# Sums of squares of an attention head: squares as stationary operand of two columns, or as moving operand of a constant

## The chip, the core and the metric

The kernel runs on one core of a Trainium2 chip. The metric is the device time of one execution in microseconds. The engines of the core are TensorE (matmul; PE and, for its weight loads, PEld in the profile), VectorE (DVE), ScalarE (ACT), GpSimd (POOL) and SyncE (SP), whose queue issues all DMAs here. Each engine works through its own instructions in the order in which the program gives them, and semaphores hold an instruction until its operands are there.

## The reference

The program is one layer of a mixer with two branches over 1152 tokens (1024 latent ones and 128 of context, nine tiles of 128). This case is about the end of the attention branch. For each of eight heads, with `va` of 128 columns a head:

```python
w = softmax(q1 @ k1.T) - lam * softmax(q2 @ k2.T)
oa = w @ v
oa = oa * lax.rsqrt(jnp.mean(jnp.square(oa), axis=-1, keepdims=True) + LN_EPS)
oa = oa * subln_g * (1.0 - lam_init)
oa = (oa * silu(za)) @ w_pa
```

The mean of squares is over the 128 columns of one head, so there is one factor per head and token.

## The kernel before

All matmul operands are float32. Most matmuls run in a faster float32 form (`F32R`), with each operand split into a rounded part (`hi_of`, a copy on ScalarE) and a remainder (`lo_of`, a subtraction on VectorE or GpSimd), and three products hi*hi, hi*lo, lo*hi. A matmul of plain float32 operands takes no split; the trace shows it as two weight loads and two matmuls.

The kernel writes its order out by hand. `Sched` (lines 38 to 136) is a planner at build time: it keeps an estimated TensorE time `sch.t` and estimated times at which ScalarE, VectorE and GpSimd come free, and runs generator streams. A stream yields the time (or a condition) at which it wants to go on; the first ready stream in the list emits its next instructions. Waits such as `yield sch.t + 4.0` only place instructions in the order; on the chip only semaphores count.

In the attention stage (`phase_b`) three streams run, in this priority: `softmax_stream`, `pv_stream`, and the dense stream. Streams that are added with `sch.spawn` go ahead of all.

- `softmax_stream` goes over the heads, in five chunks of queries each (four of 256, one of 128), in tiles of 128 queries. For both halves of the difference it writes scores into the one buffer of PSUM tag `S`, takes the maximum (line 1067, tile `nm`), then the exponential (tile `E`). `fin` combines the two halves; `eps` holds the term of each query that stands for `LN_EPS`.
- `pv_stream` (line 1106) transposes the weights of a chunk, splits them (`wTh`, `wTl`) and multiplies by V into PSUM `o`, with the head's 128 columns on partitions and queries along the free dimension. At the end of a chunk (from line 1171) it takes `Square` of `o` into `sq`, scales `o` into `o_sb`, and spawns `post`: for each 128 queries a matmul with `sq` as the stationary operand and `ones` (two columns of 1/128) as the moving one. Its result has queries on partitions, so that a copy puts it into a column of `ms`.
- `rms` (line 1080), one per head, waits for the fifth chunk, adds `eps`, takes the power -0.5 on GpSimd, transposes the nine columns to rows, stores them (`RSd`), loads them back over all partitions (`rb`, tag `rec`, two buffers, three loads of 384 queries) and scales `o_sb` with them on GpSimd. Then `done["attn", h]` is set.
- The dense stream (`dense`, line 322) takes jobs from `nxt` (line 1342): V of late heads, `z` (the gate `za` of an attention head, 12 us of matmul), `zr`, and 16 gate jobs. It loads and splits two jobs ahead. A `z` job is not placed before `done["attn", h]`; its result goes through `gate_out` (line 941): a tanh on ScalarE, a product, then on GpSimd the product with `o_sb`, then on ScalarE the split for the store. `gate_out` has two buffers `tz`, and dense jobs have two PSUM buffers `dn`. `spare` (line 1339) is the number of gate jobs that `nxt` holds back for after the last `z` job.

When the last head is scaled, `done["B"]` ends the stage. The dense stream goes on with what is left (`z` of head 7, the spare gates, then eight `pr` and eight `pa` jobs), while `x_loads` brings the `X` tiles, into the memory that the attention stage left, for the `pr` jobs.

Of the kernel before, what the change touches and what calls it, by code (L numbers as in the profile page):

```python
# [11 lines left out]
F32 = mybir.dt.float32  # L12
# [6 lines left out]
P = 128  # L19
# [3 lines left out]
NT = NL + P  # L23
# [116 lines left out]
def hybrid_step(ctx: ExitStack, tc: tile.TileContext, I: dict, O: dict):  # L140
# [5 lines left out]
    def mm(out, lhsT, rhs, start, stop):  # L146
        n = rhs.free_size()
        sch.t += max(n / 2400 + 0.013, 0.11) if lhsT.dtype == F32R else max(n / 600 + 0.01, 0.22)
        nc.tensor.matmul(out, lhsT=lhsT, rhs=rhs, start=start, stop=stop)  # L149
# [5 lines left out]
    def act(out, in_, func=AF.Copy, after=None, **kw):  # L155
        nc.scalar.activation(out, in_, func, **kw)  # L156
        extra = sum(not isinstance(v, (int, float)) for v in kw.values())
        return sch.op("act", 0.06 + out.free_size() / 1200 + 0.09 * extra, after)
# [4 lines left out]
    def v_tt(out, a, b, op, after=None):  # L163
        nc.vector.tensor_tensor(out, a, b, op=op)  # L164
        return sch.op("dve", 0.07 + out.free_size() / 960, after, in_sbuf(a, b))
# [18 lines left out]
    def p_tt(out, a, b, op, after=None):  # L184
        nc.gpsimd.tensor_tensor(out, a, b, op=op)  # L185
        return sch.op("pool", 0.2 + out.free_size() * (0.17 if op == ALU.pow else 0.00205), after, True)
# [15 lines left out]
    def dma(out, in_):  # L202
        nc.sync.dma_start(out=out, in_=in_)  # L203
# [8 lines left out]
    ONd = tc.dram_tile((NH, P, NT), F32, name="ONd")  # L212
    Gd = tc.dram_tile((16, P, NT), F32, name="Gd")
    Td = tc.dram_tile((8, P, NT), F32, name="Td")
    RSd = tc.dram_tile((NH, NTILE, P), F32, name="RSd")
    gated = tc.dram_tile((16, P), F32, name="gated")

# [12 lines left out]
    def room(tag):  # L230
        return sch.room(tag, PS[tag][1])

    def psum(tag, shape=(P, 512)):
        return PS[tag][0].tile(list(shape), F32, tag=tag, name=tag), sch.bank(tag)
# [8 lines left out]
    Y = big.tile([P, 2, KT, NT], F32R, name="Y")  # L243

    ident = const.tile([P, P], F32, name="ident")
    ones = const.tile([P, 2], F32, name="ones")
    mhalf = const.tile([P, 16], F32, name="mhalf")
    bg = const.tile([P, 16], F32, name="bg")
    bm = const.tile([P, 24], F32, name="bm")
# [109 lines left out]
    def phase_h(first, load_decays):  # L359
# [3 lines left out]
        with es:  # L363
# [42 lines left out]
            for i in range(1, NTILE):  # L406
                load_x(i)
            junk = p0.tile([P, D], mybir.dt.bfloat16, name="junk")
            nc.gpsimd.memset(ones, 1.0 / P)
            nc.gpsimd.memset(mhalf, -0.5)  # L410
            act(sc, cond, AF.Tanh, scale=0.5)
            v_stt(sc, sc, 1.0, cond, ALU.add, ALU.mult)
# [560 lines left out]
    def phase_b():  # L973
# [105 lines left out]

        def rms(h, o_sb, ms):  # L1080

            yield lambda: ms[1] if len(ms) == 2 else None
            rs = pb.tile([P, NTILE], F32, tag="rs", name="rs", bufs=2)
            f = v_tt(rs, ms[0], eps[h], ALU.add)
            yield p_tt(rs, rs, mhalf[:, :NTILE], ALU.pow, f)
            yield room("tp")
            tp, tok = psum("tp")
            tpose(tp[0:NTILE, :P], rs)
            rt = pb.tile([NTILE, P], F32, tag="rst", name="rst")
            tok[0] = act(rt, tp[0:NTILE, :P])  # L1090
            dma(RSd[h], rt)
            rb = []
            for c in range(NC):
                rb.append(pb.tile([P, CW], F32, tag="rec", name="rb", bufs=2))
                dma(rb[c], RSd[h, 3 * c:3 * c + 3].rearrange("t q -> (t q)").partition_broadcast(P))
                if c:
                    yield sch.t + (4.0 if c == 1 else 0.5)
                    for d in (c - 1, c) if c == 2 else (c - 1,):
                        if d == 2:
                            yield sch.t + 3.5  # L1100
                        cs = slice(d * CW, (d + 1) * CW)
                        f = p_tt(o_sb[:, cs], o_sb[:, cs], rb[d], ALU.mult)
            OS[h] = o_sb
            done["attn", h] = f

        def pv_stream():
# [4 lines left out]
            for h in range(NH):  # L1111
                yield lambda: 0.0 if h < 2 or ("gate_out", h - 2, True) in done else None
                o_sb = pz.tile([P, NT], F32, tag="o_sb", name="o_sb", bufs=2)
                ms = [pb.tile([P, NTILE], F32, tag="ms", name="ms", bufs=2)]
                sch.spawn(rms(h, o_sb, ms))
                for c in range(5):
                    if c == 1:
# [53 lines left out]
                    cs = slice(c * 256, c * 256 + n)  # L1171
                    yield lambda: 0.0 if state["sq"] == 0 else None
                    state["sq"] = 1
                    sq = pb.tile([P, 256], F32, tag="sq", name="sq", bufs=1)
                    act(sq[:, :n], o[:, :n], AF.Square)
                    otok[0] = act(o_sb[:, cs], o[:, :n], scale=subg)

                    def post(sq=sq, c=c, nq=nq, ms=ms, f=otok[0]):
                        yield f
                        yield room("tp")  # L1180
                        sp, tok = psum("tp")
                        for q in range(nq):
                            mm(sp[:, 2 * q:2 * q + 2], sq[:, q * P:(q + 1) * P], ones, True, True)
                        state["sq"] = 0
                        tok[0] = v_ts(ms[0][:, 2 * c:2 * c + nq], sp[:, 0:2 * nq:2], 1.0, None, ALU.mult)
                        if c == 4:
                            ms.append(tok[0])

                    sch.spawn(post())
            yield lambda: done.get(("attn", NH - 1))  # L1190
# [145 lines left out]
        zrs = list(range(NH))  # L1336
        prs = list(range(8))
        pas = list(range(8))
        spare = 2
        late_v = [4, 5, 6, 7]  # L1340

        def nxt():
# [28 lines left out]
        psum_pool(es, "tp", 2)  # L1371
        psum_pool(es, "S", 1)
        psum_pool(es, "o", 1)
        load_k(0)
        load_q(0, 0)
        sch.run([softmax_stream(), pv_stream(), stream], lambda: "B" in done)
# [251 lines left out]
```

## Time and profile before

| what | value |
|---|---|
| runs | 1703.99, 1703.97, 1699.94 us; median 1703.97 |
| profiled execution | 1701.82 us, span 1700.0 us |
| busy TensorE matmul / weight load | 97% / 95% of the span |
| busy VectorE, ScalarE, GpSimd | 50%, 36%, 48% |
| preparation and first products, 0 to 80 us | matmul busy 60.0 us |
| projections and retention, 80 to 600 us | 515.0 of 520 |
| attention with dense jobs, 600 to 1330 us | 720.7 of 730 |
| rest of dense jobs, 1389 to 1594 us | 201.7 of 205 |
| output projection, 1594 to 1700 us | 98.1 of 106 |

Views used below. The windows view has one row per stretch: its limits, its length, then busy time with number of instructions for PE, PEld, DVE, ACT and POOL, the granted TensorE clock, the busy share of the DMA engines and GB/s. The timeline has start, duration, engine, line, operation, what it writes and reads with shapes, and the number of merged instructions; in brackets stands how long the engine was idle before and who released it. Starts matter more than durations on TensorE, since matmuls overlap. The view of one tile lists the instructions that touch it, with shortest, median and longest duration in ns and the first and last start. A row of DMA issues has what it writes and reads, the number, KB each and the median time to landing.

### The profile page before, as it was taken

Reading aid. Unit: us, or ns where it says so; the run is one execution under the profiler, and the core shown is the slowest. Engines: PE = TensorE matmul, PEld = TensorE weight load, DVE = VectorE, ACT = ScalarE, POOL = GpSimd, SP = SyncE. Lnnn points to the kernel's source line nnn. Section 1 sums busy time; section 2 is a strip of 40 time slices with the busy share of each in tenths; the row PEclk is TensorE's granted clock in tenths of the full one; section 3 lists DMA queues with packets and bytes.
Section 4 is the critical chain, followed back from the end, with each engine's and each line's share of the span. In section 5 each row is a group of like instructions: output and inputs, shape, how many; then the busy total and the mean of one; then the engine's idle time right before and its main releaser. Section 6 shows DMA issues by size and latency. Waiting matters only on the chain.

```text
span 1700.0 us, 27027 instructions
## 1 busy us (share of the span) xinstructions
PE 1654.5 (97%) x10495; PEld 1609.5 (95%) x10495; DVE 856.3 (50%) x1681; ACT 609.6 (36%) x1138; POOL 813.1 (48%) x555
## 2 busy tenths in 40 slices
PE   6899999999999999999999999999999999999998
PEld 5699999999999999999999999999999999999886
DVE  8545506413714626665555665666565124134676
ACT  5632222121221235555555555555545220012200
POOL 4547417444634637664847475656656322112200
PEclk8999999999999999999999999999999999999999
DMA  7435412430341365443535353525242578854432
GB/s 274 149 100 147 131 46 86 132 116 23 100 127 44 112 204 161 152 144 113 169 97 172 92 167 93 170 95 165 75 158 73 202 273 282 260 174 137 160 125 87
DMA packets 135185, 237.36 MB, mean 140 GB/s; under 512 B 15801, under 2 KB 103313, under 8 KB 134033
## 3 DMA queue, kind: packets, MB, share of 16 engines
q1 hardware_dynamic: 135056, 235.63, 43.4%
q8 instruction: 83, 1.36, 0.3%
q14 instruction: 46, 0.37, 0.1%
HBM read 161.08 MB, written 74.49 MB: 139 GB/s over the span
## 4 chain that ended last, share of the span: by engine, by line
PE 80%; DVE 6%; DMA 5%; issue 3%; POOL 3%; ACT 2%; SPq 1%; DVEq 0%; POOLq 0%; ACTq 0%
PE dn L149 53%; PE S L149 8%; PE o L149 6%; PE e L149 6%; PE tp L153 4%; PE a L149 4%; DMA gt<-Gd 2%; DVE junk L173 1%; SPq L203 1%; DMA wm<-in_w_shift 1%; ACT E L156 1%; PE tp L149 1%; DVE st L181 1%; DVE eps L173 1%; POOL wlo L185 1%
## 5 line engine op out<-in xcount | busy, mean ns | idle before, releaser
L149 PE MATMUL dn<-Y,whi 128*128 128x384 f32 x3200 | 834.3, 341 | 8.7 <-ACT Y L156 2.8
L149 PEld LDWEIGHTS dn<-Y,whi 128*128 128x128 f32 x3200 | 568.1, 189 | 14.7 <-ACT Y L156 4.0
L149 PE MATMUL dn<-Y,wlo 128*128 128x384 f32 x1600 | 537.5, 336 | 0.7 <-DVE wlo L164 0.7
L185 POOL TENSOR_TENSOR wlo<-raw,whi 128x1024 fp32r<-128x1024 f32 x87 | 210.9, 2428 | 444.8 <-ACT whi L156 444.5
L149 PEld LDWEIGHTS dn<-Y,wlo 128*128 128x128 f32 x1600 | 301.5, 188 | 1.0 <-DVE wlo L164 1.0
L1067 DVE TENSOR_REDUCE nm<-S 128x1 f32<-128x1152 f32 x144 | 178.1, 1237 | 180.4 <-PE S L149 180.0
L189 POOL TENSOR_SCALAR E<-E,r 128x640 f32<-128x640 f32 x64 | 142.8, 2231 | 126.8 <-DVE r L173 86.2
L156 ACT ACTIVATE E<-S,nm 128x1152 f32<-128x1152 f32 x144 | 162.4, 1128 | 79.4 <-DVE nm L1067 73.5
L149 PE MATMUL dn<-whi,Y 128*128 128x256 f32 x864 | 157.4, 283 | 2.4 <-ACT rt L156 1.0
L149 PEld LDWEIGHTS dn<-whi,Y 128*128 128x128 f32 x864 | 134.1, 189 | 3.3 <-ACT rt L156 1.4
L149 PE MATMUL o<-wTh,V 128*128 128x256 f32 x576 | 133.6, 290 | 0.1
L156 ACT ACTIVATE wTh<-tp 128x512 fp32r<-128x512 f32 (+1 forms) x168 | 88.7, 544 | 111.4 <-PE tp L153 107.7
L156 ACT ACTIVATE whi<-raw 128x1024 fp32r<-128x1024 f32 x88 | 92.1, 1055 | 85.0 <-PE dn L149 84.8
L149 PE MATMUL dn<-wlo,Y 128*128 128x256 f32 x432 | 121.3, 281 | 0.0
L164 DVE TENSOR_TENSOR wTl<-tp,wTh 128x512 fp32r<-128x512 f32 (+1 forms) x168 | 99.7, 613 | 24.9 <-ACT wTh L156 24.9
L185 POOL TENSOR_TENSOR E<-E 128x640 f32<-128x640 f32 x64 | 100.9, 1576 | 5.3
L149 PE MATMUL S<-K,QH 128*128 128x384 f32 (+1 forms) x400 | 94.6, 340 | 5.8 <-ACT E L156 5.8
L149 PEld LDWEIGHTS o<-wTh,V 128*128 128x128 f32 x576 | 99.3, 188 | 0.5 <-ACT wTh L156 0.4
L149 PE MATMUL S<-K,QL 128*128 128x384 f32 (+1 forms) x400 | 92.5, 334 | 0.0
L153 PE MATMUL tp<-ident,E 128*128 128x128 f32 x584 | 86.8, 272 | 0.0
L173 DVE SCALAR_TENSOR_TENSOR gt<-gt,dn 128x384 f32<-128x384 f32 x48 | 26.6, 554 | 117.9 <-DMA gt<-Gd 64.7
L169 DVE TENSOR_SCALAR KD<-tp,kdec 128x256 f32<-128x256 f32 (+1 forms) x48 | 16.0, 408 | 138.5 <-PE tp L153 138.5
(197 smaller groups left out, 2504.4 us busy)
## 6 DMA issues: line engine op xcount, KB each, us to landing
K<-Kd SPq DMA_DIRECT2D x8, 1280.0 KB, 7.9
Gd<-gt SPq DMA_DIRECT2D x48, 192.0 KB, 2.3
V<-Vd SPq DMA_DIRECT2D x24, 384.0 KB, 3.6
gt<-Gd SPq DMA_DIRECT2D x48, 192.0 KB, 2.5
Y<-OAd SPq DMA_DIRECT2D x16, 576.0 KB, 4.2
raw<-in_w_gate SPq DMA_DIRECT2D x16, 512.0 KB, 4.0
QH<-Qh SPq DMA_DIRECT2D x64, 128.0 KB, 3.1
QL<-Ql SPq DMA_DIRECT2D x64, 128.0 KB, 2.9
```

Source lines behind the costliest of these rows:

```text
L149: nc.tensor.matmul(out, lhsT=lhsT, rhs=rhs, start=start, stop=stop)
L153: nc.tensor.transpose(out, in_, ident)
L156: nc.scalar.activation(out, in_, func, **kw)
L164: nc.vector.tensor_tensor(out, a, b, op=op)
L169: nc.vector.tensor_scalar(out, a, s1, s2, op0=op0, **kw)
L173: nc.vector.scalar_tensor_tensor(out, a, s, b, op0=op0, op1=op1, **kw)
L181: nc.vector.bn_stats(out, a)
L185: nc.gpsimd.tensor_tensor(out, a, b, op=op)
L189: nc.gpsimd.tensor_scalar(out, a, s1, None, op0=op0)
L203: nc.sync.dma_start(out=out, in_=in_)
L1067: nc.vector.tensor_reduce(nm[:, m:m + 1], ps[:, :nb, :kw], axis=AX.XY, op=ALU.max, negate=True)
```

## The change

The squares are no longer the stationary operand. `Square` goes to a float32 tile `s2`; `hi_of` and `lo_of` split it into the two halves of `sq`. `ones` becomes a 128x128 constant of 1/128 in `F32R`, made at the start of the stage, and is the stationary operand of two matmuls that accumulate into one result: every partition of it holds the row of means. One row is copied into `s2` (over the squares, which are used up) and stored to `MSd` in DRAM. The next chunk's square waits for that (`state["sq"]`, and one buffer `s2`). `rms` loads the head's row from `MSd` as nine partitions of 128, transposes it to nine columns, and goes on as before. The tags `ms` and `rst` go; `rs`, `rec` and `sq` have one buffer each, so each of the three `rb` loads of a head waits for the scaling that reads the one before it. `spare` goes from 2 to 3.

```diff
+    MSd = tc.dram_tile((NH, NT), F32, name="MSd")
...
-    ones = const.tile([P, 2], F32, name="ones")
...
-            nc.gpsimd.memset(ones, 1.0 / P)
...
         def rms(h, o_sb, ms):
 
-            yield lambda: ms[1] if len(ms) == 2 else None
-            rs = pb.tile([P, NTILE], F32, tag="rs", name="rs", bufs=2)
-            f = v_tt(rs, ms[0], eps[h], ALU.add)
+            yield lambda: ms[0] if ms else None
+            rt = pb.tile([P, CW], F32, tag="rec", name="rt")[0:NTILE, :P]
+            dma(rt, MSd[h].rearrange("(t q) -> t q", q=P))
+            yield sch.t + 3.0
+            yield room("tp")
+            tp, tok = psum("tp")
+            nc.tensor.transpose(tp[:, :NTILE], rt, ident[0:NTILE, 0:NTILE])
+            sch.t += 0.11
+            rs = pb.tile([P, NTILE], F32, tag="rs", name="rs")
+            f = tok[0] = v_tt(rs, tp[:, :NTILE], eps[h], ALU.add)
             yield p_tt(rs, rs, mhalf[:, :NTILE], ALU.pow, f)
             yield room("tp")
             tp, tok = psum("tp")
             tpose(tp[0:NTILE, :P], rs)
-            rt = pb.tile([NTILE, P], F32, tag="rst", name="rst")
+            rt = pb.tile([P, CW], F32, tag="rec", name="rt")[0:NTILE, :P]
             tok[0] = act(rt, tp[0:NTILE, :P])
             dma(RSd[h], rt)
-            rb = []
             for c in range(NC):
-                rb.append(pb.tile([P, CW], F32, tag="rec", name="rb", bufs=2))
-                dma(rb[c], RSd[h, 3 * c:3 * c + 3].rearrange("t q -> (t q)").partition_broadcast(P))
-                if c:
-                    yield sch.t + (4.0 if c == 1 else 0.5)
-                    for d in (c - 1, c) if c == 2 else (c - 1,):
-                        if d == 2:
-                            yield sch.t + 3.5
-                        cs = slice(d * CW, (d + 1) * CW)
-                        f = p_tt(o_sb[:, cs], o_sb[:, cs], rb[d], ALU.mult)
+                cs = slice(c * CW, (c + 1) * CW)
+                rb = pb.tile([P, CW], F32, tag="rec", name="rb")
+                dma(rb, RSd[h, 3 * c:3 * c + 3].rearrange("t q -> (t q)").partition_broadcast(P))
+                yield sch.t + 4.0
+                f = p_tt(o_sb[:, cs], o_sb[:, cs], rb, ALU.mult)
+                if c < NC - 1:
+                    yield f
...
-                    sq = pb.tile([P, 256], F32, tag="sq", name="sq", bufs=1)
-                    act(sq[:, :n], o[:, :n], AF.Square)
+                    s2 = pb.tile([P, 256], F32, tag="s2", name="s2")
+                    sq = pb.tile([P, 2, 256], F32R, tag="sq", name="sq")
+                    act(s2[:, :n], o[:, :n], AF.Square)
                     otok[0] = act(o_sb[:, cs], o[:, :n], scale=subg)
+                    f = hi_of(sq[:, 0, :n], s2[:, :n])
...
                         yield f
+                        yield lo_of("v", sq[:, 1, :n], s2[:, :n], sq[:, 0, :n], f)
                         yield room("tp")
                         sp, tok = psum("tp")
-                        for q in range(nq):
-                            mm(sp[:, 2 * q:2 * q + 2], sq[:, q * P:(q + 1) * P], ones, True, True)
+                        mm(sp[:, :n], ones, sq[:, 0, :n], True, False)
+                        mm(sp[:, :n], ones, sq[:, 1, :n], False, True)
+                        row = s2[0:1, :n]
+                        tok[0] = act(row, sp[0:1, :n])
+                        dma(MSd[h:h + 1, cs], row)
+                        yield tok[0] + 2.5
                         state["sq"] = 0
-                        tok[0] = v_ts(ms[0][:, 2 * c:2 * c + nq], sp[:, 0:2 * nq:2], 1.0, None, ALU.mult)
-                        if c == 4:
-                            ms.append(tok[0])
+                        if last:
+                            ms.append(sch.t)
...
-        spare = 2
+        spare = 3
...
+        ones = pb.tile([P, P], F32R, name="ones")
+        one = pb.tile([P, P], F32, tag="rec", name="one")
+        nc.gpsimd.memset(one, 1.0 / P)
+        act(ones, one)
```

More of the change, by code (lines that the diff above doesn't have):

```diff
@@ L1113, in pv_stream @@
                 o_sb = pz.tile([P, NT], F32, tag="o_sb", name="o_sb", bufs=2)
-                ms = [pb.tile([P, NTILE], F32, tag="ms", name="ms", bufs=2)]
+                ms = []
                 sch.spawn(rms(h, o_sb, ms))
@@ L1173, in pv_stream, with post @@
                     state["sq"] = 1
-                    sq = pb.tile([P, 256], F32, tag="sq", name="sq", bufs=1)
-                    act(sq[:, :n], o[:, :n], AF.Square)
+                    s2 = pb.tile([P, 256], F32, tag="s2", name="s2")
+                    sq = pb.tile([P, 2, 256], F32R, tag="sq", name="sq")
+                    act(s2[:, :n], o[:, :n], AF.Square)
                     otok[0] = act(o_sb[:, cs], o[:, :n], scale=subg)
-                    def post(sq=sq, c=c, nq=nq, ms=ms, f=otok[0]):
+                    f = hi_of(sq[:, 0, :n], s2[:, :n])
+                    def post(sq=sq, s2=s2, h=h, cs=cs, n=n, ms=ms, last=c == 4, f=f):
                         yield f
+                        yield lo_of("v", sq[:, 1, :n], s2[:, :n], sq[:, 0, :n], f)
                         yield room("tp")
                         sp, tok = psum("tp")
-                        for q in range(nq):
-                            mm(sp[:, 2 * q:2 * q + 2], sq[:, q * P:(q + 1) * P], ones, True, True)
+                        mm(sp[:, :n], ones, sq[:, 0, :n], True, False)
[4 more added lines that the diff above has]
+                        yield tok[0] + 2.5
                         state["sq"] = 0
-                        tok[0] = v_ts(ms[0][:, 2 * c:2 * c + nq], sp[:, 0:2 * nq:2], 1.0, None, ALU.mult)
-                        if c == 4:
-                            ms.append(tok[0])
+                        if last:
+                            ms.append(sch.t)
                     sch.spawn(post())
```

## The prediction

> **What bounds the kernel now.** I read the page's head first, then the windows view over the stages.
>
> ```profile
> span 1700.0 us, 27027 instructions
> 600.00:1330.00 730.00, 720.70 (x4668) 712.87 (x4668) 423.80 (x703) 382.18 (x735) 442.90 (x278) 1.00 0.43 136
> 1330.00:1389.00 59.00, 59.00 (x343) 58.91 (x342) 7.89 (x11) 15.86 (x26) 20.40 (x14) 1.00 0.71 259
> ```
>
> TensorE is the bound: 720.70 of the 730 us of the attention stage, and all of the 59 us behind it (the number behind the comma), at full clock. A microsecond of matmul removed is worth a microsecond, if nothing holds TensorE up instead. What could hold it up is the attention chain, which is beside the matmuls and not short. The view of the tile `nm` has it, with the order in which the last dense jobs are loaded:
>
> ```profile
> L1067 DVE TENSOR_REDUCE nm<-S x144: 277/1358/1360, 619.5 to 1317.0; 128x1 f32<-128x1152 f32 x128, 128x1 f32<-128x128 f32 x16
> 1301.36 0.42 SPq L203 DMA_DIRECT2D raw<-in_w_gate  x1
> 1322.02 0.42 SPq L203 DMA_DIRECT2D raw<-in_w_za  x1
> 1341.94 0.42 SPq L203 DMA_DIRECT2D raw<-in_w_gate  x1
> 1352.66 0.43 SPq L203 DMA_DIRECT2D raw<-in_w_gate  x1
> ```
>
> 144 maxima in 697.5 us is one every 4.84 us from the first to the last: scores, maximum and exponential follow one another through the one `S` buffer, so the end of attention is set by a chain of latencies, and dense jobs only fill the time between. Two jobs are always loaded ahead. The last gate before `z` of head 7 is loaded at 1301; `za` comes at 1322, with two gates (`spare`) behind it. That job may not be placed before head 7's rms chain is through. The chain as it is now:
>
> ```profile
> 1326.92 0.38 ACT L156 ACTIVATE sq<-o 128x256 f32<-128x256 f32 x1 [1.21 <-PE o L149]
> 1329.93 0.28 ACT L156 ACTIVATE sq<-o 128x128 f32<-128x128 f32 x1 [2.09 <-PE o L149]
> 1331.55 1.82 POOL L185 TENSOR_TENSOR rs<-rs,mhalf 128x9 f32<-128x9 f32 x1 [4.17 <-DVE rs L164]
> 1335.37 0.25 ACT L156 ACTIVATE rst<-tp 9x128 f32<-9x128 f32 x1
> 1335.90 0.31 SPq L203 DMA_DIRECT2D RSd<-rst  x1
> 1337.44 0.81 SPq L203 DMA_DIRECT2D rb<-RSd  x2
> 1339.49 0.58 ACT L156 ACTIVATE gt<-dn,bg 128x384 f32<-128x384 f32 x1 [3.87 <-issue]
> 1340.53 1.01 POOL L185 TENSOR_TENSOR o_sb<-o_sb,rb 128x384 f32<-128x384 f32 x1 [7.16 <-DMA rb<-RSd]
> 1345.26 1.02 POOL L185 TENSOR_TENSOR o_sb<-o_sb,rb 128x384 f32<-128x384 f32 x1 [0.39 <-DMA rb<-RSd]
> 1351.69 0.58 ACT L156 ACTIVATE gt<-dn,bg 128x384 f32<-128x384 f32 x1 [3.58 <-PE dn L149]
> 1364.18 0.49 ACT L156 ACTIVATE tz<-dn 128x384 f32<-128x384 f32 x1 [1.42 <-PE dn L149]
> 1376.65 0.58 ACT L156 ACTIVATE gt<-dn,bg 128x384 f32<-128x384 f32 x1 [3.63 <-PE dn L149]
> 1388.88 0.51 PE L149 MATMUL dn<-K,whi 128*128 128x384 f32 x2
> ```
>
> From the last Square (1329.93) to the end of the last scaling (1345.26 + 1.02 = 1346.3) it takes 16.4 us. Two gate jobs cover it: `z` 7 begins when the second ends, about 1351.7, 5.4 us after the chain. `z` 7 ends at 1364.2, each gate takes 12.5 (1376.65 - 1364.18), and the first `pr` job begins at 1388.9. That slack of 5.4 us is the number to watch.
>
> **The change: TensorE work.** A loop of the dense jobs is hi, hi, lo. What stands between two lo is read off the starts in the timeline:
>
> ```profile
> 1326.19 0.34 PE L149 MATMUL dn<-Y,wlo 128*128 128x384 f32 x1
> 1326.37 0.28 PE L149 MATMUL o<-wTh,V 128*128 128x256 f32 x1
> 1326.49 0.28 PE L149 MATMUL o<-wTl,V 128*128 128x256 f32 x1
> 1326.61 0.28 PE L149 MATMUL o<-wTh,V 128*128 128x256 f32 x1
> 1326.72 0.27 PE L153 MATMUL tp<-ident,E 128*128 128x128 f32 x1
> ...
> 1327.72 0.34 PE L149 MATMUL dn<-Y,wlo 128*128 128x384 f32 x1
> 1327.90 0.50 PE L149 MATMUL tp<-ones,sq 128*128 128x2 f32 x4
> ...
> 1328.69 0.34 PE L149 MATMUL dn<-Y,wlo 128*128 128x384 f32 x1
> ...
> 1329.21 0.34 PE L149 MATMUL dn<-Y,wlo 128*128 128x384 f32 x1
> ```
>
> An empty loop takes 0.52 (1328.69 to 1329.21), the one with four `ones` matmuls 0.97: 0.45 for a chunk of 256 queries, 0.22 for the half one. Eight heads of four chunks and a half one: 8 x (4 x 0.45 + 0.22) = 16.2 us go. In their place come two matmuls of 256 moving columns a chunk. `o<-wTh,V` has that shape and precision and starts every 0.12: 0.24 a chunk; the half chunk stays at 0.22, since a matmul with a full weight load does not get under 0.11 (1326.61 to 1326.72). So 8 x (4 x 0.24 + 0.22) = 9.4 us come. The column transpose of each head adds 8 x 0.11 = 0.9. **TensorE: -16.2 + 9.4 + 0.9 = -5.9 us**, certain as work.
>
> **Other engines.** ScalarE gains 40 times a rounding copy (nearest: 0.38, the Square of the same size) and a row copy (`rst`, 0.25); VectorE gains 40 remainders and loses 40 copies of `ms`; SP gains 40 row stores and 8 reads. None of these engines is full in the stage (424 and 382 of 730 us). What counts is where they stand in the softmax chain: all 40 x (0.38 + 0.25) = 25 us on it would be +25, none on it 0, and 0.2 us of TensorE a chunk less in its way is up to -8. I take +1, near the low end, since one link of 4.84 us waits on ScalarE only for its own exponential. The remainder reads two SBUF operands on VectorE, like this row:
>
> ```profile
> L164 DVE TENSOR_TENSOR rs<-ms,eps x8: 170/706/1527, 728.9 to 1331.3; 128x9 f32<-128x9 f32 x8
> ```
>
> The same 9 columns take 170 to 1527 ns; 1.36 us is the most that such an instruction lost here. The removed `ms` copy reads PSUM. The Trainium skill ("GPSIMD Engine Reference", section 1 Specifications) says that GpSimd shares its SBUF interfaces with VectorE, with contention for VectorE instructions with two SBUF inputs. By that rule this part of the change costs, which is the dear rival below; the spread in the row agrees with it.
>
> The setup of `ones` (a memset and a copy at the start of the stage) I cost at nothing: dense jobs cover it, as long as ScalarE isn't held for a buffer of the stage before. If it is, it costs one stop and its clock, as priced below.
>
> **The rms chain of head 7, step by step.** Square of the half chunk: it now waits until the row of chunk 3 is stored (one `s2` buffer). From 1326.92: three ScalarE steps to 1327.9, remainder 0.4 and two matmuls to 1329.0, row copy to 1329.5, and a store. `RSd` to the issue of the read behind it took 1.54 (1335.90 to 1337.44). So 1331.4 instead of 1329.93. From there: split 1.4, matmuls 0.9, row copy 0.35, store 1.6, read of the columns. The last is not in the trace; nearest are 64 KB in 2.3 us and 192 KB in 3.5:
>
> ```profile
> QH<-Qh SPq DMA_DIRECT2D x16, 64.0 KB, 2.3
> rb<-RSd SPq DMA_DIRECT2D x24, 192.0 KB, 3.5
> ```
>
> I take 2.5 with the hand-over. Sum 6.8. Transpose 0.4, sum with `eps` and power 2.2 (the power 1.82), second transpose 0.5, copy 0.4: 10.3. Store to first scaling 4.6 (1335.90 to 1340.53): 15.0. Then three scalings of 1.0; before the second and the third stands a read of 3.5 and its issue of 0.3, since `rec` has one buffer and each load waits for the scaling before it: 15.0 + 3 x 1.0 + 2 x 3.8 = **25.6 us** instead of 16.4. End: 1331.4 + 25.6 = 1357.0 instead of 1346.3.
>
> **What is queued behind it.** With `spare` 3 one gate less stands ahead of `z` 7 (the one loaded at 1301), so TensorE gets to it at 1339.5 less 5.9 = 1333.6. In TensorE's order `z` 7 stands behind both transposes, the second at 1331.4 + 9.9 = 1341.3: TensorE idles. Its matmuls need nothing of the chain and run on, 12.5 us, to 1353.8. But ScalarE meets the split of `z` 7's first third ahead of its second tanh, and that split waits for GpSimd's product with `o_sb`, which stands behind the three scalings. So the second `dn` bank comes free after 1357.0 + 1.0 (product) + 0.5 (split) + 0.5 (tanh) + 0.6 (VectorE) = 1359.6, and only then does the next gate begin. TensorE idles once more, 5.8 us. On SP, only stores of gates and the `X` loads stand behind the waiting loads of `rec`; nobody waits for them here. On ScalarE, behind the Square that waits for `s2`, stand copies of the next chunk; softmax is through by then (last maximum at 1317.0). Three gates follow, not two: 1359.6 + 37.4 = 1397.0 for the first `pr` job, against 1388.9: **+8.1 us**. The -5.9 is inside this sum; the tail has swallowed it. What follows is late by the same amount, as TensorE is full there and nothing in it changes.
>
> What a stop costs in clock:
>
> ```profile
> 609.00:612.00 3.00, 0.35 (x2) 0.35 (x2) 0.00 (x0) 0.98 (x2) 0.00 (x0) 0.82 0.93 345
> 612.00:615.00 3.00, 3.00 (x10) 3.00 (x10) 0.00 (x0) 1.09 (x2) 2.37 (x1) 0.50 0.81 215
> 615.00:618.00 3.00, 3.00 (x11) 3.00 (x11) 0.00 (x0) 0.00 (x0) 0.00 (x0) 0.54 1.05 348
> ```
>
> Matmul stands still for 3.00 - 0.35 = 2.65 us, and then the granted clock (third number from the right) is 0.50 and 0.54 for 6 us: 3 x 0.50 + 3 x 0.46 = 2.9 us lost. The stop behind `z` 7 pays that: +2.9 (the earlier stop slows only `z` 7, which waits anyway). The Trainium skill ("TensorE: Matmul & The Clock Gate", Part 1) has the clock halved after an idle window of about 3.4 us and back after as long a busy one. An estimate from that page is 1.7 us lost instead of 2.9, and nothing for stops well under 3.4 us; the row above was cold after 2.65.
>
> **Sum.** +8.1 (chain, with one gate moved behind it) + 2.9 (clock) + 1 (softmax) = +12.0. The profiled execution took 1701.8 us, 1.8 above its span and 2.2 under the median of 1703.97: **1714 us**. The last `X` load for the `pr` jobs is issued here:
>
> ```profile
> 1364.24 1.07 SPq L203 DMA_DIRECT2D X<-ORd  x2
> ```
>
> That is 19 us after the chain's end; 10.7 us later it still stands over 20 us ahead of the first `pr` job, so it adds nothing.
>
> **The rivals.**
> *Whole gain (faster).* If the chain does not decide, only -5.9 is left: 1696. For that the last Square must come early enough: the first `pr` job at 1388.9 - 5.9 = 1383.0 needs it by 1383.0 - 37.4 - 2.6 - 25.6 = 1317.4 instead of 1331.4. That is 14 us over 144 links, 0.1 us a link. For it: the links are far from uniform, and less `ones` work is in their way. Against it: nothing shortens a link directly, and ScalarE gets more. 0.16.
> *Partly covered (no change).* The chain is shorter than my 25.6, or attention ends some 4 to 10 us sooner: 1699 to 1709. DMA waits are the largest part of the 25.6, so this is near. 0.27.
> *Dear (slower still).* The remainders wait for GpSimd and lengthen the softmax chain: 0.25 us a chunk is 10 us, all of it passed on to the tail: about 1724. 0.12.
> *Forecast*, 1709 to 1720: 0.45.
>
> **The numbers.** About 0.3% (5 us) is what this measurement can tell from no change. Faster 0.16, same 0.27, slower 0.45 + 0.12 = 0.57. The range takes in the whole gain at its lower end and the dear rival at its upper: 1696 to 1724.
>
> **What would show it.** Right: TensorE waits before the column transpose of head 7, then a second stop with low clock between `z` 7 and the next gate; the last scaling some 25 us behind the last Square; one gate evacuated less before `z` 7, three after. The mean start distance of the row matmuls 0.12. Wrong: no stop behind head 7 and the first `pr` job before 1384; or maxima that end well before 1317 or well after 1320; or TensorE waits at each head's column transpose, which I cost at nothing since at the other heads filler stands there.

## The result, and the profile after

The kernel after takes **1744.57 us** (median of 4 runs, 1740.93 to 1745.99); the kernel before, run beside it, took 1702.27. The ratio is 1.0246, 95% interval 1.0231 to 1.026: 42 us slower. The forecast of 1714 had the direction and missed the size by 30 us; 1744.57 lies outside the range of 1696 to 1724. The direction is in part luck: the stops that the forecast was added up from, at head 7, did not come (see below).

The windows view of the kernel after, with the two stretches of the prediction first (limits, length, busy us of PE, PEld, DVE, ACT, POOL, granted clock, DMA share, GB/s):

```profile
600.00:1330.00 730.00, 692.05 (x4387) 675.52 (x4386) 427.75 (x704) 397.71 (x804) 437.84 (x275) 0.98 0.41 130
1330.00:1389.00 59.00, 56.56 (x325) 55.55 (x323) 4.00 (x6) 13.55 (x22) 21.73 (x15) 1.00 0.68 248
```

TensorE stands still for 730 - 692.05 = 38.0 us of the attention stage, where it was 9.3 before, and its clock is 0.98 in place of 1.00. Over the whole span the mean clock is 0.986 (before 0.994). That makes the balance: 1743.5 x 0.014 = 24.4 us lost to the clock against 1700.0 x 0.006 = 10.2; gaps between matmuls from 600 us on, added up from the timeline, 43.9 us against 12.8. +14.2 + 31.1 - 5.9 (the work that went) = +39.4 of the 43.5 us between the spans. The balance is rough: the clock has three digits, which leaves up to 1.7 us open, and some of the time at the low clock is gap and counted in both terms. So the question is not what TensorE does more, but what it waits for. The waits view does not say: its largest new lines are small.

```profile
PE S L149 <- ACT E L156: 12.3, 9, 2.8
PE dn L149 <- ACT gt L156: 8.1, 3, 4.3
...
PE tp L149 <- DVE sq L164: 4.6, 2, 3.3
```

(us in total, times, longest.) The stalls are spread over attention matmuls, which is what one sees when the other work, the filler, has run out. The windows view restricted to the dense jobs' tile `dn` shows that it has:

```profile
831.00:853.00 22.00, 0.00 (x0) 0.00 (x0) 0.56 (x1) 0.01 (x1) 0.84 0.31 92
925.00:948.00 23.00, 0.00 (x0) 0.00 (x0) 0.00 (x0) 0.09 (x1) 0.93 0.29 84
1102.00:1121.00 19.00, 0.00 (x0) 0.00 (x0) 0.00 (x0) 0.00 (x0) 1.00 0.28 88
1198.00:1210.00 12.00, 0.00 (x0) 0.00 (x0) 0.00 (x0) 0.41 (x1) 0.65 0.28 83
```

The first two busy columns (PE, PEld) are zero: four stretches, 76 us in all, without one dense matmul; before had none over 4.4 us. The same stretches with all tiles show that attention alone fills only two thirds of TensorE:

```profile
831.00:853.00 22.00, 15.66 (x92) 14.50 (x93) 10.83 (x16) 10.61 (x21) 13.46 (x10) 0.84 0.31 92
925.00:948.00 23.00, 15.26 (x88) 13.33 (x86) 13.91 (x20) 13.83 (x28) 16.17 (x11) 0.93 0.29 84
...
1198.00:1210.00 12.00, 7.49 (x27) 6.47 (x28) 7.40 (x11) 6.28 (x12) 7.59 (x5) 0.65 0.28 83
```

What ends the first stretch stands in the timeline of the kernel after, head 1:

```profile
813.32 0.28 ACT L156 ACTIVATE s<-o 128x128 f32<-128x128 f32 x1 [2.51 <-DMA MSd<-s]
...
817.91 0.24 SPq L203 DMA_DIRECT2D MSd<-s  x1
...
830.09 0.34 PE L149 MATMUL dn<-Y,wlo 128*128 128x384 f32 x1
...
835.65 1.01 POOL L185 TENSOR_TENSOR o_sb<-o_sb,rb 128x384 f32<-128x384 f32 x1
...
842.72 1.00 POOL L185 TENSOR_TENSOR o_sb<-o_sb,rb 128x384 f32<-128x384 f32 x1
...
846.86 1.01 POOL L185 TENSOR_TENSOR o_sb<-o_sb,rb 128x384 f32<-128x384 f32 x1 [3.13 <-DMA rb<-RSd]
...
853.10 0.59 PE L149 MATMUL dn<-Y,whi 128*128 128x384 f32 x2
...
861.62 0.52 ACT L156 ACTIVATE tz<-dn 128x384 f32<-128x384 f32 x1
```

The last dense matmul is at 830.09, the next at 853.10, and its result goes to a `tz`: it is `z` of head 1. `z` may not be placed before `done["attn", 1]`, and the last scaling of `o_sb` ends at 847.87; the planner's order puts the first matmul of `z` 5.2 us behind that. From the Square of the half chunk (813.32) that is 34.6 us: the row is stored only at 817.91, and the three scalings stand 7.1 and 4.1 us apart, each behind its own load into the one `rec` buffer. Before, the same chain stood like this:

```profile
812.52 0.28 ACT L156 ACTIVATE sq<-o 128x128 f32<-128x128 f32 x1 [0.33 <-PE o L149]
...
832.40 1.02 POOL L185 TENSOR_TENSOR o_sb<-o_sb,rb 128x384 f32<-128x384 f32 x1
...
833.78 0.49 ACT L156 ACTIVATE tz<-dn 128x384 f32<-128x384 f32 x1 [3.03 <-PE dn L149]
...
838.70 0.49 ACT L156 ACTIVATE tz<-dn 128x384 f32<-128x384 f32 x1 [1.86 <-POOL gol L185]
```

20.9 us, and the scaling ends (833.42) as the last third of `z` 0 is evacuated (833.78); `z` 1 goes on without a stop. There was no spare time at this head. Measured in this way, from the Square of the half chunk to the end of the last scaling, the chain takes 21.9 us in the mean of the eight heads before and **39.9** after. It is the quantity to follow through the experiments: below, "chain" is this mean.

### The profile page after: what moved, and what is told of

It is laid out like the page before. It is cut to its first block, busy times and chain, and to the rows that moved or that the text cites. A ratio compares the mean times of both kernels' runs of the same rounds, so it can differ in the third digit from the quotient of the medians.

```text
span 1743.5 us, 27113 instructions
## 1 busy us (share of the span) xinstructions
PE 1664.5 (95%) x10439; PEld 1611.7 (92%) x10439; DVE 861.2 (49%) x1681; ACT 633.1 (36%) x1220; POOL 815.7 (47%) x555
## 4 chain that ended last, share of the span: by engine, by line
PE 79%; DVE 6%; DMA 6%; ACT 3%; issue 2%; POOL 2%; SPq 1%; DVEq 0%; POOLq 0%; ACTq 0%
PE dn L149 52%; PE S L149 7%; PE o L149 6%; PE e L149 5%; PE tp L153 4%; PE a L149 4%; DVE junk L173 2%; ACT E L156 1%; DMA MSd<-s 1%; DVE nm L1066 1%; DMA wm<-in_w_shift 1%; SPq L203 1%; POOL wlo L185 1%; DMA X<-ORd 1%; DMA gt<-Gd 1%
## 5 line engine op out<-in xcount | busy, mean ns | idle before, releaser
L189 POOL TENSOR_SCALAR E<-E,r 128x640 f32<-128x640 f32 x64 | 146.5, 2288 | 120.1 <-DVE r L173 91.5
L153 PE MATMUL tp<-ident,E 128*128 128x128 f32 x584 | 91.1, 279 | 7.0 <-DVE wTl L164 3.6
L149 PE MATMUL o<-wTl,V 128*128 128x256 f32 x288 | 82.8, 287 | 3.8 <-DVE wTl L164 3.7
```

The lines of the kernel that those rows point to most:

```text
L153: nc.tensor.transpose(out, in_, ident)
L189: nc.gpsimd.tensor_scalar(out, a, s1, None, op0=op0)
```

## The experiments

The theory that came out of the traces is called GATE in the first expectations and LENGTH in the later ones: the longer chain holds `z` back, dense work runs out, TensorE idles and its clock falls. Its rivals are named in each expectation. Every kernel was timed against the kernel before on the same chip; the ratios are to those runs.

| kernel | edit | chain, us | time, us | ratio (95%) |
|---|---|---|---|---|
| before | | 21.9 | 1702 to 1704 | 1 |
| after | | 39.9 | 1744.6 | 1.0246 (1.0231 to 1.026) |
| e1 | after, `z` asked for later | 40.5 | 1736.2 | 1.0205 (1.0185 to 1.0225) |
| e3 | before, mark 12 us late | 22.6 (+12 in the order) | 1724.5 | 1.0135 (1.0119 to 1.015) |
| e10 | before, mark 20 us late | 22.1 (+20 in the order) | 1732.9 | 1.0184 (1.0156 to 1.0212) |
| e4 | before, more work on ScalarE and VectorE | 22.4 | 1705.1 | 1.0017 (1.0004 to 1.003) |
| e5 | before, one `rec` buffer | 31.1 | 1720.4 | 1.0105 (1.0086 to 1.0124) |
| e16 | before, sums through DRAM | 29.1 | 1724.8 | 1.0142 (1.0112 to 1.0172) |
| e9 | before, both | 40.7 | 1744.2 | 1.0247 (1.022 to 1.0274) |
| e7 | after, `z` not behind the chain | 40.2 | 1716.1 | 1.0081 (1.0059 to 1.0103) |
| e8 | before, `z` not behind the chain | 22.3 | 1704.6 | 1.0007 (0.9992 to 1.0021) |
| e13 | after, half chunk has its own buffer | 41.0 | 1747.8 | 1.0265 (1.0231 to 1.0299) |
| e11 | e7 and that buffer | 41.1 | 1714.0 | 1.0062 (1.0045 to 1.0079) |
| e12 | e11 with other times in the order | 42.3 | 1719.2 | 1.0097 (1.0077 to 1.0117) |
| e14 | after, squares not split, two `rec` | 28.8 | 1749.3 | 1.0259 (1.0237 to 1.0282) |
| e15 | e14, half chunk has its own buffer | 29.7 | 1725.2 | 1.0139 (1.0109 to 1.0169) |

**e1: `z` asked for later.** In after `z` is loaded once its head's attention has come to the third chunk, so that it stands right behind a gate that is not open yet. In e1 it is loaded at the fifth chunk.

```diff
-                    if c == (2 if h + 1 < NH else 4):
+                    if c == 4:
                         done["z", h] = True
```

> The changed kernel, but every z job becomes ready for the dense stream only at the fifth chunk of its head (heads 0 to 6: at the third chunk until now), some 25 us later, so that its head's rms chain is through when its turn comes. Theory GATE (the longer rms chain keeps z jobs shut, the dense stream stands still behind them in the middle of attention, and TensorE has only attention left): no stretch over 8 us without a dense matmul between 640 and 1330 us, and most of the 42 us gone: 1697 to 1715 us. Theory ENGINES (the added copies, remainders and DMA waits lengthen the attention work itself on the chip): 1735 to 1750 us, as the changed kernel.

1736.2: GATE's number was missed, and the time lies in the range of ENGINES. The long stretches without dense work went (the longest left is 7.7 us), but the gaps still add up to 42.1 us: the stops moved to other places (TensorE stood 5.7 us for one transpose of the chain itself, behind `rs` on GpSimd), and the half chunk of head 7 came at 1343.5 and not at 1328.7. Taking a waiting job out of the way is worth 8 us; the lateness itself stays.

**e3 and e10: the order alone.** Nothing that a chip executes is added; only the mark is set 12 or 20 us later in the planner's time.

```diff
+            yield sch.t + 12.0
             OS[h] = o_sb
             done["attn", h] = f
```

> The kernel before, with one line more: done['attn', h] is set 12 us later on the planner's clock. No instruction is added, and nothing waits longer on the chip; only the order in which instructions are placed differs. GATE: stretches of about 10 us without dense matmuls appear at the heads whose z job had no slack (1, and 4 or 6), 1712 to 1740 us. ENGINES: 1700 to 1708 us, as before.

> The kernel before with 20 us, not 12 as in e3, between the last scaling of o_sb and the mark that lets z of that head be placed; nothing that a chip executes is added. LENGTH with a loss that grows with each microsecond at each head where z stands directly behind the mark (heads 1, 2, 4, 5, 6 and 7 by now): 8 us more than in e3 at four to six heads, of which the stream makes up about half, so 1737 to 1755. ONCE (a late head moves the stream once, and the later heads find their slack again): e3's 1724 plus 8 us at most, 1724 to 1733.

1724.5 and 1732.9. On each engine stands the same work (but for two and three copies fewer on ScalarE, which the planner leaves out where it takes the other form of the tanh's product), and 23 and 30 us are lost, by the mark that comes late in the order: for `z` at every head, and at head 7 for the end of the stage as well. e3 lies in the range of GATE. The windows view of e10, dense tile only, has stretches of the same kind as after:

```profile
836.00:852.00 16.00, 0.00 (x0) 0.01 (x1) 0.56 (x1) 0.29 (x1) 0.79 0.26 89
1274.00:1289.00 15.00, 0.00 (x0) 0.00 (x0) 0.00 (x0) 0.00 (x1) 0.83 0.21 67
```

For 8 us more delay the loss grew by 7.5, at the upper edge of ONCE: a head's lateness is made up in part before the next one.

**e4: the work alone.** In the chunk's path of the kernel before, a copy of 128x256 and a copy of a row on ScalarE, and on VectorE a maximum of `sq` with itself in place of the subtraction, are added; the values stay as they are.

```diff
+                    act(sq[:, :n], sq[:, :n])
+                    f = act(sq[0:1, :n], sq[0:1, :n])
...
+                        yield v_tt(sq[:, :n], sq[:, :n], sq[:, :n], ALU.max, f)
```

> The kernel before, with the added work of the split alone: per chunk one copy of the squares on ScalarE, one copy of a row, and on VectorE one 128x256 operation with two SBUF operands, all in place and without effect on values. The rms chain grows by about 1.3 us. GATE: 1702 to 1710 us. ENGINES: 1715 to 1745 us, with the link between two maxima longer than 4.84 us.

1705.1, +0.17% (at most 0.3%): ENGINES falls. The split's instructions cost some 3 us, at most 5.

**e5, e16, e9: the two parts of the longer chain, put into the kernel before.** e5 takes after's loop over `rb` with one `rec` buffer. e16 sends the nine columns of sums to DRAM and back. e9 has both. The sums are made by the old small matmuls. The trip in e9 (in e16 `back` has two buffers):

```diff
-            f = v_tt(rs, ms[0], eps[h], ALU.add)
+            dma(MSd[h], ms[0])
+            yield sch.t + 2.5
+            back = pb.tile([P, CW], F32, tag="rec", name="back")[:, :NTILE]
+            dma(back, MSd[h])
+            yield sch.t + 3.0
+            f = v_tt(rs, back, eps[h], ALU.add)
```

> The kernel before, with the loads of the factors through one buffer, as in the changed kernel: load, scaling, load, scaling, load, scaling. It lengthens the rms chain by about 5 of the 9 us that the change adds behind the power. GATE: part of the stops, 1705 to 1725 us. ENGINES: 1700 to 1706 us.

> The kernel before with one thing put in: the nine columns of sums go to DRAM and back, as in e9, but the rows of rstd keep their two buffers. No row is made and no buffer of squares is held. LENGTH: the chain is some 6 to 8 us longer than before, as in e5, so 1713 to 1726. PLACE (the loss is not set by how long the chain is but by where its waits fall in the order: any trip through DRAM costs the whole 40 us, as in e14): 1736 to 1750.

> The kernel before, its sums of squares still made by the four small matmuls with ones, but with both parts that lengthen the rms chain put in: the nine columns of sums go to DRAM and back before eps is added, and the rows of rstd come back one after another through one rec buffer. LENGTH (the length of the chain alone makes the loss, whatever the sums are made with): e5 with the one buffer took +19 us for about +8 us of chain, the trip adds some 6 to 7 us of chain more, so 1733 to 1748, with stretches of 10 us and more without a dense matmul behind heads 1, 2, 4 and 5. SQUARES (a good part of the loss comes from the new way of making the sums: remainders on VectorE, s2 held until its row is stored): 1718 to 1728, little over e5.

1720.4, 1724.8 and 1744.2. This is the result on which the argument rests: +18.8 for one buffer, +22.6 for the trip, +41.6 for both, and the whole loss of the change is +42.3. The change's own new sums are not in e9, and it is as slow as after. That the two losses agree so closely is in part chance: after has 5.9 us of matmul less than e9, so some 6 us of its loss come from something else. The 3 us of e4 may be a part of them. The windows view of e9, dense tile only, has stretches of the same kind, behind heads 1, 2, 5 and 6 (behind head 4 there is one of 9.6 us):

```profile
833.00:848.00 15.00, 0.00 (x0) 0.00 (x0) 0.55 (x1) 0.05 (x1) 0.77 0.37 122
929.00:948.00 19.00, 0.00 (x0) 0.00 (x0) 0.00 (x0) 0.68 (x2) 0.82 0.32 104
1192.00:1204.00 12.00, 0.00 (x0) 0.00 (x0) 0.00 (x0) 0.45 (x1) 1.00 0.27 91
1279.00:1290.00 11.00, 0.00 (x0) 0.00 (x0) 0.00 (x0) 0.38 (x2) 0.89 0.35 119
```

**e7 and e8: take `z` out from behind the chain.** The scaling by rstd and the gate are both products, so they can be done in either order. In e7 the gate of `z` is the last `o_sb` of the head and not the chain. Where `z` comes first, silu(z) is multiplied into `o_sb` in place (`gate_z`), and the scaling, the split and the stores come behind it (`z_out`). The chain stays as long as in after. e8 is the same edit on the kernel before.

```diff
-            return Job("W", [I["w_za"][h]], y_of, evac, gate=lambda: done.get(("attn", h)))
+            return Job("W", [I["w_za"][h]], y_of, evac, gate=lambda: done.get(("o", h)))
...
+                if c == 4:
+                    OS[h] = o_sb
+                    done["o", h] = otok[0]
...
+                z = ("zp", h, c) in done
+                if z:
+                    yield lambda: done.get(("zm", h, c))
+                else:
+                    done["sc", h, c] = True
                 f = p_tt(o_sb[:, cs], o_sb[:, cs], rb, ALU.mult)
...
+                if z:
+                    z_out(c, o_sb[:, cs], h)
```

> The kernel after, but the z job of a head waits only for the last chunk of its attention and not for the rms chain: where z is evacuated first, its silu is multiplied into o_sb in place, and the scaling by rstd, the split and the stores come behind it. The chain itself stays as long as in after. LENGTH through the gate of z: the stretches without a dense matmul go, 1698 to 1712; with TensorE's work 5.9 us less it may even pass the kernel before. TAIL (the lateness only moves to the next consumer of the chain: o_sb is freed later for head h+2, and the products wait on GpSimd): 1725 to 1745.

> The same rearrangement of z, on the kernel before with its old sums of squares and its short chain. LENGTH: the chain of before was covered at nearly all heads, so little is to be had: 1694 to 1704. TAIL: the extra steps behind the chain cost, 1704 to 1715. e7 less e8 is what the changed sums are worth when z does not stand behind the chain: LENGTH -6 to +8, TAIL +20 or more.

1716.1 and 1704.6. With a chain of 40.2 us, as long as after's, two thirds of the loss are gone (28.5 of 42.3 us), and the same edit does nothing where the chain is short. e7 lies between its two expectations, and so does e7 less e8, 11.5 us. No stretch without dense work over 5.7 us is left in it; what is left are stops of another kind:

```profile
909.74 0.28 ACT L156 ACTIVATE s<-o 128x128 f32<-128x128 f32 x1 [4.70 <-DMA MSd<-s]
...
1382.87 1.06 ACT L156 ACTIVATE junk<-o_sb 128x1024 f32<-128x1024 f32 x1 [9.44 <-DMA o_sb<-in_cond_rows]
```

ScalarE works in order: the first line is the Square of a half chunk that waits until the row of chunk 3 has been stored from the one buffer `s2`; exponentials queue behind it. The second is not of the change: the rows of the condition are asked for among the loads of `X`.

**e13, e11, e12: the held row.** e13 is after with a buffer of its own for the half chunk's squares (a constant of 2 columns, not 128, makes room; for chunk 4 the planner waits for the two matmuls and the row's copy alone; the small tile `r` has a buffer less). e11 is the same on e7, and the `junk` (the silu of the condition) is placed 12 us, not 4, behind its load. e12 then changes three times in the order.

```diff
-                    s2 = pb.tile([P, 256], F32, tag="s2", name="s2")
+                    s2 = pb.tile([P, n], F32, tag="s2" if lat else "s2b", name="s2")
...
-        ones = pb.tile([P, P], F32R, name="ones")
+        ones = pb.tile([P, 2], F32R, name="ones")
```

> The kernel after, with nothing changed but that the half chunk of a head has a buffer of its own for its squares, and that the constant has 2 columns instead of 128 to make room. In after ScalarE stood 8.3 us at four heads until the row of chunk 3 was stored. HELD ROW (this wait is a main part of the loss): 1744 less 8.3 of waits and up to as much again of clock and late chains, 1728 to 1736. LENGTH (the length of the chain in front of z is nearly all of it; the held row adds at most its own 2 to 3 us to a chain of 34 to 40): 1735 to 1744.

> e7 with three waits less. The half chunk of a head gets a buffer of its own for its squares (room for it comes from a constant of 2 columns instead of 128), so that ScalarE no longer holds its exponentials back until the row of chunk 3 is stored (4.70, 3.30 and 5.36 us in e7, at three heads); and the silu of the condition waits 12 us, not 4, for its rows, which in e7 held ScalarE for 9.4 us and TensorE for 5.7. LENGTH, with the held row as the second cost of the change: the three stops of 2.6, 2.0 and 3.8 us and that of 5.7 go, with one or two of their spells at half clock (2.9 each): 1716 - 14 - 5 = 1697 to 1705, and the 5.9 us of TensorE work would show at last. TAIL (what e7 still loses is the chain of head 7, some 15 us longer than before, ahead of the split of the last z): 1708 to 1714.

> e11 with three times of the order changed: the transpose of the columns of sums is placed 5.5 us, not 3, behind its load (TensorE stood up to 2.8 us for it), the rows of the condition are asked for 4.5 us sooner, ahead of most loads of X, and their silu waits 5 us for them instead of 12, as it moved VectorE work of e11 into the pr jobs. LENGTH: e11's 1714 less some 3 us of waits in the attention stage and some 5 us behind it: 1702 to 1708, no faster than the kernel before by more than can be told. TAIL (longer waits in the order only push the chain of each head back): 1711 to 1718.

1747.8, 1714.0 and 1719.2. In after the held row costs nothing that shows: ScalarE stood 8.3 us for it in all, and without it e13 is no faster (it is 4 us above the upper expectation, with runs from 1741 to 1754). That the long chain hides it is likely, but not shown. Nor does e11 gain what was expected; TAIL had the right number. Its gaps are 25.7 us from 600 us on, still twice those of before, and some of them are new (VectorE's work on the condition now meets the `pr` jobs). In e12 the chain of one head came to 58.6 us, and the time is above both expectations; three things changed at once, so which of them did it is open. None of these kernels beats the kernel before: with `z` out of the chain's way, the 5.9 us saved on TensorE are still more than given back. Which of the many small stops of e11 make up its last 10 us was not settled.

**e14 and e15: the new rows with a short chain.** The squares are not split: one plain float32 matmul makes the row. That frees room for two `rec` buffers and the old loop; the trip through DRAM stays.

```diff
-                        yield lo_of("v", sq[:, 1, :n], s2[:, :n], sq[:, 0, :n], f)
...
-                        mm(sp[:, :n], ones, sq[:, 0, :n], True, False)
-                        mm(sp[:, :n], ones, sq[:, 1, :n], False, True)
+                        mm(sp[0:2, :n], ones, s2[:, :n], True, True)
```

> The kernel after with the trip of the sums through DRAM as its only delay: the squares are not split (one float32 matmul with 2 constant columns makes the row, about as long on TensorE as the four small ones of before), and the room that this frees gives the rows of rstd their two buffers and the loop of before back. LENGTH: the chain is some 7 to 9 us longer than before and not 17, about what the one buffer made in e5 (1720), so 1713 to 1728; e9, with both, was 1744, so the two parts add up or a little over. OTHER (it is the rows and their in-order waits for DRAM that cost, the buffer little on top of them): 1732 to 1744.

> e14 with a buffer of its own for the squares of the half chunk. In e14 no long stretch without dense matmuls is left but one of 11.9 us; ScalarE stood 24.7 us, at five heads, for the store of the row of chunk 3, and TensorE 13.3 us behind it. HELD ROW (in e14 this wait took the place of the chain): 13 us of stops and about four spells of half clock at 2.9 us go, 1715 to 1728. PLACE (the stops only move to the next in-order wait, as they did in e13): 1736 to 1750.

e14 took 1749.3, and LENGTH failed on it: a chain of 28.8 us, and as slow as after. Only one long stretch without dense work is in its trace. The view of the tile `MSd` in e14 names another wait:

```profile
  ACT s L156: 24.7, 5
```

(us, times.) Chunk 4 follows close behind chunk 3 there, and ScalarE stands at five heads, 24.7 us in all, until the row is stored. TensorE stops behind it, in its own order, for up to 4.85 us:

```profile
1199.13 0.38 PE L149 MATMUL tp<-s,ones 128*2 128x128 f32 x2 [4.85 <-ACT s L156]
```

e15 gives the half chunk its own buffer, with the shorter wait of the planner as in e13, and takes 1725.2, 24 us less: the number of HELD ROW. So the held row is a second cost. It is worth 24 us at a chain of 29 us (e14 less e15) and nothing that can be told at 40 (after and e13). e15 takes as long as e16, which sends columns through DRAM and makes no rows at all, but not for the same reasons: its plain float32 matmul takes TensorE longer than was expected, some 11 us in all (worked out in the last section), so these two runs do not show that the trip costs the same with either kind of sum.

## Why the prediction was wrong

*TensorE work.* Right in size: the row of a chunk now takes 0.23 us for both matmuls (predicted 0.24):

```profile
660.81 0.39 PE L149 MATMUL tp<-sq,ones 128*128 128x256 f32 x2
661.04 0.51 PE L149 MATMUL dn<-Y,whi 128*128 128x384 f32 x2
```

The half chunk adds 0.22 to a dense loop, as predicted, but the reason given, that no matmul with a full weight load gets under 0.11, does not hold: at 911.52 its two matmuls take 0.17 together (the next one starts at 911.69). No run shows the 5.9 us as time.

*Softmax and the other engines.* Right in that the added work alone is worth little (e4). But the sum has softmax 1 us later, and the last maximum is at 1311.8, 5.2 us sooner than before (1317.0); why was not tested.

```profile
L1066 DVE TENSOR_REDUCE nm<-S x144: 278/1358/1359, 619.7 to 1311.8; 128x1 f32<-128x1152 f32 x128, 128x1 f32<-128x128 f32 x16
```

The dear rival (remainders that wait for GpSimd) happens, but at few places: TensorE stood 4.6 us in all for `sq` from VectorE, in two stops (the third line of the waits view above). More on it below.

*The chain of head 7.* The mechanism was right and the size too small: 30.6 us from the Square (1328.73 to 1359.36) where 25.6 was predicted.

```profile
1328.73 0.27 ACT L156 ACTIVATE s<-o 128x128 f32<-128x128 f32 x1
...
1338.90 1.82 POOL L185 TENSOR_TENSOR rs<-rs,mhalf 128x9 f32<-128x9 f32 x1 [7.60 <-DVE rs L164]
...
1341.91 0.25 ACT L156 ACTIVATE rt<-tp 9x128 f32<-9x128 f32 x1
...
1348.52 1.01 POOL L185 TENSOR_TENSOR o_sb<-o_sb,rb 128x384 f32<-128x384 f32 x1 [4.03 <-DMA rb<-RSd]
...
1358.34 1.02 POOL L185 TENSOR_TENSOR o_sb<-o_sb,rb 128x384 f32<-128x384 f32 x1 [1.26 <-DMA rb<-RSd]
```

The power starts 10.2 us behind the Square (predicted 7.6), the first scaling 19.8 (15.0). Each hand-over between engines was some tenths longer than I took, and both reads behind a store were longer. The end is 1359.4 where 1357.0 was predicted; the Square came earlier than expected.

***The step that failed: what the chain holds up at the other heads.*** The prediction priced the longer chain at head 7 alone, "since at the other heads filler stands there". The filler is not there: the dense stream is one queue in order, and when its next job is a `z` whose gate is shut, the gate jobs behind that `z` cannot pass. I had the slack of `z` 7 in a row (5.4 us) and did not ask for that of the other heads, where it was 0.4 us at head 1 (833.42 to 833.78). The rows of head 1 before, shown above, say that a longer chain must stop TensorE there. e9 shows that it does, e7 that two thirds of the loss go through the gate of `z`, e3 and e10 that the late place in the order is enough for a loss of this kind. In after it happens at heads 1, 2, 4 and 5. The stops at head 7 from which the sum was made, +8.1 and +2.9 for the clock behind them, did not come.

*The clock, counted once.* One stop and +2.9 us were in the sum. There are many stops, and the clock takes 14.2 us more than before. In the first stretch, the two longest stops in the timeline, and then the clock in rows of 5 us each:

```profile
832.27 0.86 PE L149 MATMUL S<-K,QH 128*128 128x384 f32 x3 [1.84 <-ACT E L156]
...
838.71 0.38 PE L149 MATMUL o<-wTh,V 128*128 128x256 f32 x1 [2.91 <-ACT wTh L156]
```

```profile
830.00:835.00 5.00, 3.16 (x15) 2.74 (x14) 1.80 (x3) 2.65 (x4) 4.92 (x4) 0.78 0.46 125
835.00:840.00 5.00, 1.75 (x8) 1.15 (x7) 3.32 (x7) 2.81 (x5) 4.81 (x4) 0.84 0.56 177
840.00:845.00 5.00, 4.66 (x28) 4.46 (x27) 1.55 (x3) 1.58 (x3) 3.64 (x4) 0.69 0.13 47
```

The granted clock falls to 0.69 by 840 to 845 us, though no stop of this stretch is longer than 2.91 us (the first number in the brackets). The Trainium skill ("TensorE: Matmul & The Clock Gate", Part 1) ties the half clock to an idle window of about 3.4 us; here stops below that pay it too. Not each of them does: in the third stretch above (1102 to 1121) TensorE stood 2.42 us for the scores at 1107.23 and the clock stayed at 1.00, while behind the stop of 1.84 us it is down to 0.78. The length of one stop does not decide it; what does is not shown here.

*`spare` and what follows head 7.* Void. The prediction had three gates behind `z` 7. In the timeline of SP there are five:

```profile
1328.28 0.42 SPq L203 DMA_DIRECT2D raw<-in_w_za  x1
...
1341.48 0.42 SPq L203 DMA_DIRECT2D raw<-in_w_gate  x1
...
1354.83 0.42 SPq L203 DMA_DIRECT2D raw<-in_w_gate  x1
...
1368.80 0.35 SPq L203 DMA_DIRECT2D raw<-in_w_gate  x1
...
1382.76 0.45 SPq L203 DMA_DIRECT2D raw<-in_w_gate  x1
...
1398.89 0.42 SPq L203 DMA_DIRECT2D raw<-in_w_gate  x1
...
1411.40 0.38 SPq L203 DMA_DIRECT2D raw<-in_w_pr  x1
```

By then the stream is late by the gates that it could not run, so `spare` holds nothing back; with `spare` at 2 the program has the same instructions in the same order on every engine. TensorE does not idle at head 7's transposes either (the timeline has no gap over 0.1 us from 1326 to 1382), since two gates loaded earlier stand in front of `z` 7. A stop behind `z` 7 exists (4.26 us at 1386.85), but by another cause: ScalarE waits for the condition's rows among the loads of `X`. The first `pr` job begins at 1435.1 and not at 1397.0.

*The chances.* "Slower" had 0.57, and the range ended where the dear rival did. What came true had neither a chance nor a price. Nearest to it is "TensorE waits at each head's column transpose", among the things that would make the prediction wrong; but in after TensorE has no wait at that transpose in its waits view. It stops in attention, since the filler is gone. With the row of head 1 in hand this was worth a chance and a price.

## What to carry to other kernels

When a change lengthens a latency chain, list every consumer behind the chain with its slack, not only the last one: a job queue in fixed order has no filler behind a job whose gate is shut. A new trip through DRAM, or one buffer where there were two, adds next to nothing to any engine's busy time and can still cost several times the matmul time that is saved: each was worth about 20 us here, against 5.9. Putting only that into the old kernel (e9) is a cheap way to see it. If a product commutes, gate the matmul on what it needs and put the late factor behind it (e7); here that gave back two thirds of the loss.

## What the hardware showed that was not expected

A VectorE subtraction with two operands in SBUF took 2.38 us where its median is 0.42, beside one on GpSimd. VectorE, then GpSimd, in the timeline of after:

```profile
1200.62 2.38 DVE L164 TENSOR_TENSOR sq<-s,sq 128x256 fp32r<-128x256 f32 x1
```

```profile
1200.38 2.34 POOL L185 TENSOR_TENSOR wlo<-raw,whi 128x1024 fp32r<-128x1024 f32 x1 [5.33 <-ACT whi L156]
```

It ends 0.3 us after GpSimd's does, as if it had been held for all of it, and TensorE stopped 3.26 us for its result. Of the 32 such subtractions over 256 columns in this trace, eight took 0.6 us or more, and each of the eight ran beside an instruction of GpSimd; none of those that ran beside none took over 0.43. Running beside one is not enough, though: others did so for up to 0.4 us and were not slowed. The Trainium skill ("GPSIMD Engine Reference", section 1 Specifications) speaks of contention on the shared SBUF interfaces for such instructions; the trace agrees, and shows how large it can be.

One plain float32 matmul of 256 columns with a constant of 2 columns takes TensorE longer than two F32R ones with 128. In the timeline of e14:

```profile
699.24 0.34 PE L149 MATMUL dn<-Y,wlo 128*128 128x384 f32 x1
699.51 0.59 PE L149 MATMUL tp<-s,ones 128*2 128x256 f32 x2
700.04 0.61 PE L149 MATMUL dn<-Y,whi 128*128 128x384 f32 x2
700.48 0.34 PE L149 MATMUL dn<-Y,wlo 128*128 128x384 f32 x1
```

The start behind it comes 0.53 us later, against the 0.23 above. From one lo to the next it takes 1.24 us, where an empty loop takes 0.52: 0.72 more, against 0.45 for the four small matmuls of before. For the half chunk it is 0.51 against 0.23. In eight heads that is 8 x (4 x 0.27 + 0.28), about 11 us of matmul that e14 and e15 have on top of the kernel before.
